# Matmul, GELU, matmul on one Trainium2 core: the first product, too, partly from seven half-size products, with its sums shared out to accumulating DMAs

## Chip, core and metric

The kernel runs on one core of one Trainium2 chip. The metric is device microseconds for one execution; where several runs of a kernel are shown, their median. Inputs and output lie in the chip's main memory (HBM) as float32.

## What is computed

```python
m, k, n, p = 1024, 1024, 2048, 1024          # a: m x k, b: k x n, c: n x p
h = np.matmul(a, b)
h = 0.5 * h * (1 + np.tanh(np.sqrt(2 / np.pi) * (h + 0.044715 * h ** 3)))
return np.matmul(h, c).astype(np.float32)
```

Two products of 1024 x 1024 x 2048 multiply-adds each, with a GELU between them. In the text `h` is the matrix after GELU. Its transpose is what the kernel makes and keeps: `n` on the partitions, `m` along the free dimension, so that it can be the weights of the second product without another transpose.

## The kernel before

TensorE multiplies a 128x128 weight tile by a moving tile of 128 rows and up to 512 columns into PSUM; eight such steps of the contraction over `k`, or over half of `n`, give one 128x512 result. [...] The order on every engine is the order of the program text.

**First product.** `a` is cut into two halves of 512 rows (h = 0, 1). Half 0 arrives through SyncE's queue in four tiles (L74-79), is cast to bf16 by VectorE and ScalarE, and is transposed on TensorE into `aT[0]` (L111-120). The first 768 columns of `b` (`W0`, six tiles of 128) arrive on the same queue, eight loads of 128 rows, 384 KB each (L81-86), into a ring of eight float32 buffers (`b0stage`), and are cast half by VectorE, half by ScalarE (L124-126). L136-143 run over the eight rows of `b` as they arrive, six results side by side in six banks. Everything else comes through GpSimd's queue, which casts float32 to bf16 on the way: a tiny copy on GpSimd that reads the fifth `b` load (`gate`, L94) holds these loads back until then. They are the remaining columns of `b`, the second half of `a`, and `c`. `mm1(t, h)` (L167-172) computes one 128x512 tile of `h` with eight matmuls and has ScalarE apply the GELU from PSUM. In all the first product is 2 x 16 x 8 = 256 matmuls with 512 columns, all bf16. Half 1 of `a` is transposed by `turn(j)` (L185-190) between the last tiles of half 0.

**Second product.** It is already made of seven half-size products instead of eight (the Winograd form of Strassen's method). `h` is seen as 2x2 blocks `h11 h12 / h21 h22` (first index: half of `m`, second: half of `n`), `c` as `c11 c12 / c21 c22`. Sums of blocks take the place of blocks:

- of `h`: `s1 = h21 + h22`, `s2 = s1 - h11`, `s3 = h11 - h21`, and later `s4 = h12 - s2`, in the room of `s2`;
- of `c`: `t1 = c12 - c11`, `t2 = c22 - t1`, `t3 = c22 - c12`, and later `t4 = t2 - c21`, in the room of `t2`.

Each of the seven products is four rows (j) of eight matmuls. Sums are kept in the type float32r (`F32R`), which TensorE multiplies from four-byte data; blocks that need no sum are bf16. All sums are VectorE `tensor_tensor` instructions, issued during the sixteen tiles `mm1(t, 1)` (L235-249) and between the rows of products (L256-259, L263, L266). The order of the products is `h11 c11`, `h12 c21` (three of its four rows), `s2 t2`, `s3 t3`, `s1 t1`, `s4 c22`, `h22 t4`, and at the end the fourth row of `h12 c21` in three narrow pieces. PSUM results are added up by VectorE into `u2` and `u3` and stored through SyncE's queue (`combine`, L294-297).

Of the kernel before, what the change touches and what calls it, by code (L numbers as in the profile page):

```python
# [9 lines left out]
F32 = mybir.dt.float32  # L10
BF16 = mybir.dt.bfloat16
# [8 lines left out]
def kernel(ctx, tc, a, b, c, out):  # L20
    nc = tc.nc
# [8 lines left out]
    W0 = N0 * 128  # L30
    N1 = 4
    W1 = N1 * 128

# [9 lines left out]
    b0stage = ctx.enter_context(tc.tile_pool(name="b0stage", bufs=8))  # L43
# [9 lines left out]
    NH = NT // 2  # L53
    aT = [keep.tile([128, KT, H], BF16, name=f"aT{h}", tag=f"A{h}") for h in range(2)]
    WB = W0 + W1
    b_lo = keep.tile([128, KT, WB], BF16, name="b_lo", tag="B0")
    b_hi = keep.tile([128, KT, N - WB], BF16, name="b_hi", tag="B1")

    def bcols(k0, kn, n0, w):
        if n0 < WB:  # L60
            return b_lo[:, k0:k0 + kn, ds(n0, w)]
        return b_hi[:, k0:k0 + kn, ds(n0 - WB, w)]

    def bt(k, t):
        return bcols(k, 1, t * 128, 128)[:, 0, :]


    hq = [[keep.tile([128, NH, H], F32R if h else BF16, name=f"h{h}{g}") for g in range(2)]
          for h in range(2)]
# [19 lines left out]
    for mt in range(4):  # L89
        load_a0(mt, 2 if mt == 3 else 1)  # L90
# [38 lines left out]
    for mt in range(4):  # L129
        if mt < 3:  # L130
            ab.append(cast_a0(mt + 1))
        turn0(mt, ab[mt], (0,) if mt == 3 else (0, 1))
        if mt < 3:
            warm_up(3)
    cast_b0(0)
    for k in range(KT):  # L136
        if k + 1 < KT:
            cast_b0(k + 1)
        for t in range(N0):
            nc.tensor.matmul(ps[t], bt(k, t), aT[0][:, k, :],  # L140
                             start=(k == 0), stop=(k == KT - 1))
        if k == 0:
            turn0(3, ab[3], (1,))

    def gelu(t, h, p):
        nc.scalar.activation(hq[h][t // NH][:, t % NH, :], p, AF.Gelu_apprx_tanh)  # L146

    for t in range(N0):
        gelu(t, 0, ps[t])


    def load_b(k0, kn, n0, w):
        nc.gpsimd.dma_start(out=bcols(k0, kn, n0, w), in_=bv[:, k0:k0 + kn, ds(n0, w)])

    ps = [(tpool if t < 2 else ppool).tile([128, H], F32, name="pt" if t < 2 else "ps")
          for t in range(N1)]
    for k in range(0, KT, 4):
        load_b(k, 4, W0, W1)
        for i in range(4):
            for t in range(N1):  # L160
                nc.tensor.matmul(ps[t], bt(k + i, N0 + t), aT[0][:, k + i, :],  # L161
                                 start=(k + i == 0), stop=(k + i == KT - 1))
    for t in range(N1):
        gelu(N0 + t, 0, ps[t])


    def mm1(t, h):  # L167
        p = ppool.tile([128, H], F32, name="ps")
        for k in range(KT):
            nc.tensor.matmul(p, bt(k, t), aT[h][:, k, :],  # L170
                             start=(k == 0), stop=(k == KT - 1))
        gelu(t, h, p)

    W2 = 384
    for n0 in range(W0 + W1, N, W2):
        for k in range(0, KT, 4):
            load_b(k, 4, n0, W2)

    a1 = []
    for j in range(4):  # L180
        st = abf.tile([128, K], BF16, name="ab1")
        nc.gpsimd.dma_start(out=st, in_=av[:, 4 + j, :])
        a1.append(st)

    def turn(j):  # L185
        ab = a1[j]
        pt = tpool.tile([128, KT, 128], BF16, name="pt")
        for k in range(KT):
            nc.tensor.transpose(pt[:, k, :], ab[:, ts(k, 128)], ident)  # L189
        nc.vector.tensor_copy(aT[1][:, :, ts(j, 128)], pt)  # L190

    for t in range(N0 + N1, NT):
        mm1(t, 0)
        if t == NT - 3:
            turn(0)
        if t == NT - 2:
            turn(1)
            turn(2)
            turn(3)
# [7 lines left out]
    (h11, h12), (h21, h22) = hq  # L207
    c11 = keep.tile([128, NH, H], BF16, name="c11")
    c21 = keep.tile([128, NH, H], BF16, name="c21")
    c22 = keep.tile([128, NH, H], F32R, name="c22")  # L210
    c12 = keep.tile([128, NH, H], BF16, name="c12", tag="A0")
# [5 lines left out]
    load_c(c11, 0, 0)  # L217
    load_c(c22, 1, 1)
    load_c(c21, 1, 0)
    load_c(c12, 0, 1)  # L220

    t1 = [astage.tile([128, 2, H], F32R, name="t1", tag="a_st") for _ in range(4)]
    t2 = [b0stage.tile([128, 1, H], F32R, name="t2", tag="b0_st") for _ in range(8)]
    s1 = keep.tile([128, NH, H], F32R, name="s1")

    def sum_t1(i):
        nc.vector.tensor_tensor(t1[i], c12[:, ts(i, 2), :], c11[:, ts(i, 2), :], op=SUB)  # L227

    def sum_t2(t):
        nc.vector.tensor_tensor(t2[t], c22[:, t:t + 1, :], t1[t // 2][:, t % 2:t % 2 + 1, :], op=SUB)  # L230

    def sum_s1(t):
        nc.vector.tensor_tensor(s1[:, t, :], h21[:, t, :], h22[:, t, :], op=ADD)

    for t in range(NT):  # L235
        mm1(t, 1)
        if 3 <= t < 7:
            sum_t1(t - 3)
        if 6 <= t < 10:
            sum_t2(2 * (t - 6))  # L240
            sum_t2(2 * (t - 6) + 1)
        if t == WB // 128:
            t3 = keep.tile([128, NH, H], F32R, name="t3", tag="B0")
        if t >= NH + 1:
            sum_s1(t - NH - 1)
        if WB // 128 <= t < WB // 128 + 4:
            i = t - WB // 128
            nc.vector.tensor_tensor(t3[:, ts(i, 2), :], c22[:, ts(i, 2), :], c12[:, ts(i, 2), :], op=SUB)
    sum_s1(NH - 1)

    s2 = [keep.tile([128, NH // 2, H], F32R, name=f"s2{g}", tag=f"A{g}") for g in range(2)]

    def pair(x, i):
        return x[i // 2][:, ts(i % 2, 2), :]

    for i in range(4):  # L256
        nc.vector.tensor_tensor(pair(s2, i), s1[:, ts(i, 2), :], h11[:, ts(i, 2), :], op=SUB)
    for i in range(4):
        nc.vector.tensor_tensor(h21[:, ts(i, 2), :], h11[:, ts(i, 2), :], h21[:, ts(i, 2), :], op=SUB)
    s3 = h21  # L260

    def sum_s4(i):
        nc.vector.tensor_tensor(pair(s2, i), h12[:, ts(i, 2), :], pair(s2, i), op=SUB)  # L263

    def sum_t4(t):
        nc.vector.tensor_tensor(t2[t], t2[t], c21[:, t:t + 1, :], op=SUB)  # L266

    def bank(w=H):
        return ppool.tile([128, w], F32, name="ps", padded_shape=[128, H])

    def prod(p, lhs, rhs, j, q=slice(0, H)):
        for t in range(NH):
            nc.tensor.matmul(p, lhs(t)[:, ts(j, 128)], rhs(t)[:, q],  # L273
                             start=(t == 0), stop=(t == NH - 1))

    def whole(x):
        return lambda t: x[:, t, :]
# [4 lines left out]
    def pairs(x):  # L282
        return lambda t: x[t // 2][:, t % 2, :]

    def ones(x):
        return lambda t: x[t][:, 0, :]

    def new_out():
        return opool.tile([128, H], F32, name="ot")

# [3 lines left out]
    def combine(m, q, p, u, op=ADD, swap=False):  # L294
        ot = new_out()
        nc.vector.tensor_tensor(ot, u if swap else p, p if swap else u, op=op)  # L296
        store(ot, m, q * H)

    R = range(4)
    u2 = [abf.tile([128, H], F32, name="u2", tag="ab1") for _ in R]  # L300
    u3 = keep.tile([128, 4, H], F32, name="u3", tag="B1")

    for j in R:
        p = bank()
        prod(p, whole(h11), whole(c11), j)
        nc.scalar.activation(u2[j], p, AF.Copy)  # L306
    for j in range(3):
        p = bank()
        prod(p, whole(h12), whole(c21), j)
        combine(j, 0, p, u2[j])  # L310
    last = u2[3]
    last_keep = opool.tile([128, H], F32, name="lk", bufs=1)
    nc.gpsimd.tensor_copy(last_keep, last)  # L313
    for j in R:
        p = bank()
        prod(p, halves(s2), ones(t2), j)
        nc.vector.tensor_tensor(u2[j], p, u2[j], op=ADD)
    for j in R:
        p = bank()
        prod(p, whole(s3), whole(t3), j)  # L320
        nc.vector.tensor_tensor(u3[:, j, :], p, u2[j], op=ADD)
        sum_s4(j)
    for j in R:
        p = bank()
        prod(p, whole(s1), pairs(t1), j)
        combine(4 + j, 1, p, u3[:, j, :])
        nc.vector.tensor_tensor(u2[j], p, u2[j], op=ADD)
        sum_t4(2 * j)
        sum_t4(2 * j + 1)
    for j in R:  # L330
        p = bank()
        prod(p, halves(s2), whole(c22), j)
        combine(j, 1, p, u2[j])
    for j in R:
        p = bank()
        prod(p, whole(h22), ones(t2), j)
        combine(4 + j, 0, p, u3[:, j, :], op=SUB, swap=True)
    for q0, w, queue in ((0, 256, nc.sync), (256, 128, nc.scalar), (384, 128, nc.sync)):
        p = bank(w)
        prod(p, whole(h12), whole(c21), 3, q=ds(q0, w))  # L340
        ot = new_out()
        nc.vector.tensor_tensor(ot[:, 0:w], p, last_keep[:, ds(q0, w)], op=ADD)  # L342
# [30 lines left out]
```

## Time and profile before

| | us |
|---|---|
| three runs | 123.58, 123.93, 124.08 |
| median | 123.93 |
| the profiled execution, whole | 123.87 |
| its span, first to last instruction in the profile | 122.1 |

The granted TensorE clock was 1.0 for the whole span. The profile counts the busy time of each engine, but matmuls are pipelined, so "TensorE busy" is not "TensorE at its peak"; the pace at which matmuls follow each other is read from the chain of waits and from the timeline. Three stretches of the span will be spoken of:

| stretch, us from the span's start | what runs | matmuls of 512 columns |
|---|---|---|
| 0 to 21.85 | loads, casts, transposes, first six tiles of `h` | 48 |
| 21.85 to 69.02 | rest of the first product | 208, and 32 transposes |
| 69.02 to 119.2 | second product | 224 (the last eight in 24 narrower pieces) |

The time after 119.2 is the last sum and the store of its result.

### The profile page before, as it was taken

To read this page: it belongs to the slowest core of one execution; us is meant where nothing else is said; L and a number is where in the kernel's file an instruction comes from. 1 tells how busy PE (TensorE), PEld (TensorE's weight loads), DVE (VectorE), ACT (ScalarE), POOL (GpSimd) and SP (SyncE) were. 2 spreads that over 40 slices of the span, in tenths; PEclk is the share of its full clock that TensorE was granted. 3 is DMA by queue.
4 is the path that set the end of the run, shared out by engine and by line. 5 is a ranking of instruction groups with operands and counts; after the bars stand their busy time and mean duration, and the time that the engine had idled before them with its cause. 6 is when DMAs were issued, how large, how long until landed. Compare 5 with 4: busy or idle time off the path is not lost.

```text
span 122.1 us, 1486 instructions
## 1 busy us (share of the span) xinstructions
PE 116.1 (95%) x577; PEld 68.3 (56%) x577; DVE 64.6 (53%) x95; ACT 30.7 (25%) x54; POOL 21.5 (18%) x26
## 2 busy tenths in 40 slices
PE   6977999999998999999999999999999999999990
PEld 2542444444456444444444444468888888888880
DVE  0352340000014200006999999999769999974351
ACT  4454752806331133233323331100000000000000
POOL 2000099132440220000000000797000000000000
PEclk9999999999999999999999999999999999999999
DMA  3999969999999999995000000000600022445425
GB/s 144 351 328 347 413 188 191 198 200 205 209 207 206 329 394 231 206 206 97 0 0 0 5 0 3 3 0 0 258 0 0 5 86 86 157 167 191 163 99 167
DMA packets 12582, 18.44 MB, mean 151 GB/s; under 512 B 800, under 2 KB 7584, under 8 KB 12576
## 3 DMA queue, kind: packets, MB, share of 16 engines
q0 software_dynamic: 7968, 8.91, 39.6%
q1 hardware_dynamic: 4464, 9.37, 20.9%
q10 hardware_dynamic: 144, 0.07, 0.2%
q8 instruction: 4, 0.07, 0.2%
q14 instruction: 2, 0.02, 0.0%
HBM read 20.97 MB, written 4.19 MB: 206 GB/s over the span
## 4 chain that ended last, share of the span: by engine, by line
PE 88%; DMA 6%; SPq 2%; DVE 1%; ACT 0%; issue 0%
PE ps L273 41%; PE ps L170 31%; PE ps L140 8%; DMA b_st<-in_b_dram 6%; PE ps L161 3%; PE pt L161 3%; SPq L78 2%; PE pt L189 1%; DVE aT L190 1%; ACT b_lo L126 0%; SPq L85 0%; DVE ot L342 0%; PE pt L115 0%
## 5 line engine op out<-in xcount | busy, mean ns | idle before, releaser
L146 ACT ACTIVATE h<-ps 128x512 fp32r<-128x512 f32 (+1 forms) x30 | 17.3, 602 | 28.6 <-PE ps L170 26.3
L170 PE MATMUL ps<-aT,b_hi 128*128 128x512 bf16 x96 | 21.4, 379 | 0.0
L170 PE MATMUL ps<-aT,b_lo 128*128 128x512 bf16 x80 | 17.4, 379 | 0.0
L170 PEld LDWEIGHTS <-b_hi 128*128 128x128 bf16 x96 | 9.3, 98 | 10.8
L273 PE MATMUL ps<-t,s 128*128 128x512 f32 x64 | 15.0, 392 | 0.0
L273 PE MATMUL ps<-t,h 128*128 128x512 f32 x64 | 14.8, 389 | 0.0
L273 PE MATMUL ps<-c,h 128*128 128x512 bf16 (+2 forms) x80 | 14.2, 336 | 0.0
L313 POOL COPY lk<-u 128x512 f32<-128x512 f32 x1 | 7.7, 7684 | 33.6 <-ACT u L306 33.6
L273 PEld LDWEIGHTS ps<-t,s 128*128 128x128 f32 x64 | 12.0, 188 | 2.6
L273 PEld LDWEIGHTS ps<-t,h 128*128 128x128 f32 x64 | 12.0, 188 | 2.5
L170 PEld LDWEIGHTS <-b_lo 128*128 128x128 bf16 x80 | 7.8, 98 | 9.4
L227 DVE TENSOR_TENSOR t<-c,c 128x1024 fp32r<-128x1024 bf16 x4 | 4.7, 1222 | 15.8 <-DMA c<-in_c_dram 15.7
L190 DVE COPY aT<-pt 128x1024 bf16<-128x1024 bf16 x4 | 2.7, 689 | 19.4 <-PE pt L189 19.3
L140 PE MATMUL ps<-aT,b_lo 128*128 128x512 bf16 x48 | 10.9, 380 | 0.8 <-DVE b_lo L125 0.8
L273 PEld LDWEIGHTS <-h 128*128 128x128 bf16 x80 | 7.2, 98 | 7.0 <-issue 0.3
L140 PEld LDWEIGHTS <-b_lo 128*128 128x128 bf16 x48 | 4.5, 98 | 6.6 <-DVE b_lo L125 1.1
L215 POOL DMA_DIRECT2D c<-in_c_dram x8 | 5.9, 744 | 11.7 <-PE ps L170 6.0
L296 DVE TENSOR_TENSOR ot<-ps,u 128x512 f32<-128x512 f32 x11 | 7.3, 684 | 1.1 <-PE ps L273 1.1
L101 PE MATMUL ps<-warm 128*128 128x512 bf16 x17 | 6.3, 516 | 1.2 <-DVE warm L49 1.2
L273 PE MATMUL ps<-c,s 128*128 128x512 f32 x32 | 7.4, 389 | 0.0
L273 PEld LDWEIGHTS ps<-c,s 128*128 128x128 f32 x32 | 6.0, 188 | 1.2
L125 DVE CAST b_lo<-b_st 128x384 bf16<-128x384 f32 x8 | 2.9, 368 | 5.1 <-DMA b_st<-in_b_dram 5.1
(40 smaller groups left out, 96.5 us busy)
## 6 DMA issues: line engine op xcount, KB each, us to landing
out_dram<-ot SPq DMA_DIRECT2D x15, 256.0 KB, 2.0
c<-in_c_dram POOLq DMA_DIRECT2D x6, 512.0 KB, 14.8
b_st<-in_b_dram SPq DMA_DIRECT2D x7, 384.0 KB, 8.1
c<-in_c_dram POOLq DMA_DIRECT2D x2, 1024.0 KB, 15.0
a_st<-in_a_dram SPq DMA_DIRECT2D x3, 512.0 KB, 4.1
b_hi<-in_b_dram POOLq DMA_DIRECT2D x4, 384.0 KB, 11.3
b_lo<-in_b_dram POOLq DMA_DIRECT2D x2, 512.0 KB, 7.2
ab<-in_a_dram POOLq DMA_DIRECT2D x4, 256.0 KB, 13.9
```

The costliest lines, as they stand in the source:

```text
L101: nc.tensor.matmul(ps[N0 - 1], warm[:, 0:128], warm, start=True, stop=True)
L125: nc.vector.tensor_copy(b_lo[:, k, 0:HW], b_st[k][:, 0:HW])
L140: nc.tensor.matmul(ps[t], bt(k, t), aT[0][:, k, :], start=(k == 0), stop=(k == KT - 1))
L146: nc.scalar.activation(hq[h][t // NH][:, t % NH, :], p, AF.Gelu_apprx_tanh)
L161: nc.tensor.matmul(ps[t], bt(k + i, N0 + t), aT[0][:, k + i, :], start=(k + i == 0), stop=(k + i == KT - 1))
L170: nc.tensor.matmul(p, bt(k, t), aT[h][:, k, :], start=(k == 0), stop=(k == KT - 1))
L190: nc.vector.tensor_copy(aT[1][:, :, ts(j, 128)], pt)
L215: nc.gpsimd.dma_start(out=dst[:, t:t + 4, :], in_=cv[:, r * NH + t:r * NH + t + 4, ts(q, H)])
L227: nc.vector.tensor_tensor(t1[i], c12[:, ts(i, 2), :], c11[:, ts(i, 2), :], op=SUB)
L273: nc.tensor.matmul(p, lhs(t)[:, ts(j, 128)], rhs(t)[:, q], start=(t == 0), stop=(t == NH - 1))
L296: nc.vector.tensor_tensor(ot, u if swap else p, p if swap else u, op=op)
L313: nc.gpsimd.tensor_copy(last_keep, last)
```

## The change

The half of `h` that belongs to the first 1024 columns of `b` (`h11`, `h21`) is still computed directly, with 64 + 64 matmuls. The other half (`h12`, `h22`) is computed as a 2x2 block product of its own: `a` in halves of `m` and of `k`, the last 1024 columns of `b` in halves of `k` and of `n`. With `bx` for the left two of these four blocks and `b12`, `b22` for the right two, it takes seven products of four rows with four matmuls each, 112 matmuls where there were 128. Its sums are `as1`, `as2`, `as3` (of `a`), `bt2`, `bt3` and the new `b12` (of `b`), all float32r; `a22` is a float32r copy of a block of `aT[1]`, made by ScalarE. The GELU now follows a VectorE sum (`add_gelu`) for these tiles. The core of the diff, first product:

```diff
-    W0 = N0 * 128
+    W0 = N // 2
-    b0stage = ctx.enter_context(tc.tile_pool(name="b0stage", bufs=8))
+    b0stage = ctx.enter_context(tc.tile_pool(name="b0stage", bufs=6))
...
+    nc.gpsimd.dma_start(out=b12, in_=bv[:, 0:KH, W0 + H:N])
+    nc.gpsimd.dma_start(out=b22, in_=bv[:, KH:KT, W0 + H:N])
+    for k in range(0, KT, KH):
+        nc.gpsimd.dma_start(out=bx[:, k:k + KH, :], in_=bv[:, k:k + KH, W0:W0 + H])
...
+        nc.scalar.activation(a22[:, :, ts(j, 128)], aT[1][:, KH:KT, ts(j, 128)], AF.Copy)
...
+    def mm1_half(t, q):
+        p = bank(256)
+        for k in range(KT):
+            nc.tensor.matmul(p, b_lo[:, k, ts(t, 128)], aT[1][:, k, ts(q, 256)],
+                             start=(k == 0), stop=(k == KT - 1))
+        gelu(h21[:, t, ts(q, 256)], p)
...
+    mm1(6, 0, h11[:, 6, :])
+    turn(0)
+    mm1(7, 0, h11[:, 7, :])
+    turn(1)
+    turn(2)
+    mm1_half(0, 0)
+    turn(3)
+    mm1_half(1, 0)
+    mm1_half(2, 0)
+    for t in range(3):
+        mm1_half(t, 1)
...
+    for i in range(2):
+        tt(as1[i], aT[1][:, P2[i], :], aT[1][:, P2[i + 2], :], op=ADD)
...
+    for t in range(3, NH):
+        mm1(t, 1, h21[:, t, :])
...
+    def add_gelu(dst, p, u):
+        ot = new_out()
+        tt(ot, p, u, op=ADD)
+        gelu(dst, ot)
...
+    for j in R:
+        p = bank()
+        prod(p, KH, whole(bx), whole(aT[0]), j)
+        nc.scalar.activation(v2[:, j, :], p, AF.Copy)
+    for j in R:
+        p = bank()
+        prod(p, KH, whole(bx, KH), whole(aT[0], KH), j)
+        add_gelu(h12[:, j, :], p, v2[:, j, :])
+        if j >= 2:
+            sum_t1(j - 2)
+    for j in R:
+        p = bank()
+        prod(p, KH, pairs(bt2), pairs(as2), j)
+        tt(v2[:, j, :], p, v2[:, j, :], op=ADD)
+        if j >= 2:
+            sum_t1(j)
+    for i in range(2):
+        nc.gpsimd.dma_start(out=as2[i], in_=aT[0][:, P2[i + 2], :], accum_op=ADD)
+    for i in range(2):
+        nc.gpsimd.dma_start(out=bt2[i], in_=bx[:, P2[i + 2], :], accum_op=ADD)
+    for j in R:
+        p = bank()
+        prod(p, KH, pairs(bt3), pairs(as3), j)
+        tt(v3[j], p, v2[:, j, :], op=ADD)
...
+    def sum_t2(i):
+        nc.scalar.mul(t2[i], c22[:, P2[i], :], -1.0)
+        nc.gpsimd.dma_start(out=t2[i], in_=t1[:, P2[i], :], accum_op=ADD)
...
+        prod(p, KH, whole(b12), pairs(as1), j)
+        add_gelu(h22[:, 4 + j, :], p, v3[j])
+        tt(v2[:, j, :], p, v2[:, j, :], op=ADD)
...
+        prod(p, KH, whole(b22), pairs(as2), j)
+        add_gelu(h12[:, 4 + j, :], p, v2[:, j, :])
...
+        prod(p, KH, pairs(bt2), whole(a22), j)
+        add_gelu(h22[:, j, :], p, v3[j])
```

`sum_t2(0)` and `(1)` stand ahead of the product `b12 as1`, `sum_t2(2)` and `(3)` after it, `sum_s1(2)` and `(3)` ahead of the last of the seven, `sum_s1(0)` and `(1)` after it.

In the second product the seven products are the same, in another order, and four groups of its sums move from VectorE to DMAs that GpSimd issues and that add their source to what lies in the destination (`accum_op=ADD`), after ScalarE has written the other operand, negated, where the sum is a difference. Signs are chosen so that every such sum is an addition:

```diff
+    for j in R:                                  # p1
+        prod(p, NH, whole(h11), whole(c11), j)
+        nc.scalar.activation(p1[:, j, :], p, AF.Copy)
+    for i in (2, 3, 0, 1):
+        nc.scalar.mul(t3p(i), c12[:, P2[i], :], -1.0)
+        nc.gpsimd.dma_start(out=t3p(i), in_=c22[:, P2[i], :], accum_op=ADD)
+    c21 = keep.tile([128, NH, H], BF16, name="c21", tag="BX")
+    load_c(c21, 1, 0)
+    for j in R:                                  # p5
+        prod(p, NH, pairs(s1), whole(t1), j)
+        nc.scalar.activation(p5[:, j, :], p, AF.Copy)
...
+    for j in R:                                  # p6
+        prod(p, NH, halves(s2), pairs(t2), j)
+        tt(u2[:, j, :], p, p1[:, j, :], op=ADD)
+        tt(p5[:, j, :], u2[:, j, :], p5[:, j, :], op=ADD)
+    for g in range(2):
+        nc.gpsimd.dma_start(out=s2[g], in_=h12[:, ts(g, KH), :], accum_op=ADD)
+    for i in R:
+        nc.gpsimd.dma_start(out=t2[i], in_=c21[:, P2[i], :], accum_op=ADD)
+    for j in R:                                  # p7
+        prod(p, NH, whole(s3), t3t, j)
+        tt(u3[j], p, u2[:, j, :], op=ADD)
+        combine(4 + j, 1, p, p5[:, j, :])
+    for j in range(3):                           # p2
+        prod(p, NH, whole(h12), whole(c21), j)
+        combine(j, 0, p, p1[:, j, :])
+    for j in R:                                  # p3
+        prod(p, NH, halves(s2), whole(c22), j)
+        combine(j, 1, p, p5[:, j, :])
+    for j in R:                                  # p4
+        prod(p, NH, whole(h22), pairs(t2), j)
+        combine(4 + j, 0, p, u3[j])
```

(The names p1 to p7 beside the loops are added here, and the lines that take a bank are left out.) `c21` is loaded only now, into the room of `bx`; before, it was loaded with the rest of `c`. The last row of `h12 c21` in three pieces stays at the end, and GpSimd's copy `lk` (L313) is gone.

## The prediction

> **What bounds the kernel now.** I read the chain that ended last first, by engine and then in order of time, because it says which engine a saved microsecond must come from.
>
> ```profile
> PE 88%; DMA 6%; SPq 2%; DVE 1%; ACT 0%; issue 0%
> ...
> 12.62 9.23 PE ps L140 x42
> ...
> 37.83 0.46 PE pt L189 x8
> 38.30 0.02 issue
> 38.32 0.70 DVE aT L190
> 39.02 0.04 issue
> 39.06 0.61 PE pt L189 x8
> 39.67 29.35 PE ps L170 x136
> 69.02 50.17 PE ps L273 x240
> ```
>
> The reader sees a TensorE that is fed without a gap from 12.62 on, but for 0.7 us at a transpose. A bf16 matmul of 512 columns costs 29.35 / 136 = 0.216 us. So the number of matmuls is the time, and fewer of them is a gain only if nothing else becomes late. Second, the stages of the second product, 32 matmuls each (window, TensorE busy first, DMA share and GB/s last):
>
> ```profile
> 80.76:88.23 7.47, 7.47 (x35) 6.17 (x33) 7.02 (x10) 0.00 (x0) 3.91 (x1) 1.00 0.28 105
> 88.23:95.48 7.25, 7.25 (x33) 6.01 (x32) 5.93 (x7) 0.00 (x0) 0.00 (x0) 1.00 0.00 0
> 95.48:102.73 7.25, 7.25 (x33) 6.01 (x32) 7.25 (x12) 0.00 (x0) 0.00 (x0) 1.00 0.20 75
> ```
>
> Float32r matmuls take 7.25 / 32 = 0.2266 us. VectorE is nearly full here, DMA nearly idle. Third, the loads at the start and VectorE's pitch, from the timeline, and the DMA rate of one window (last number, GB/s):
>
> ```profile
> 15.15 0.38 POOL L94 COPY gate<-b_st 128x1 f32<-128x1 f32 x1 [13.84 <-DMA b_st<-in_b_dram]
> 15.46 1.63 POOL L153 DMA_DIRECT2D b_lo<-in_b_dram  x2
> 17.04 0.36 DVE L125 CAST b_lo<-b_st 128x384 bf16<-128x384 f32 x1 [0.53 <-DMA b_st<-in_b_dram]
> 18.01 0.36 DVE L125 CAST b_lo<-b_st 128x384 bf16<-128x384 f32 x1 [0.61 <-DMA b_st<-in_b_dram]
> ...
> 98.10 0.68 DVE L327 TENSOR_TENSOR u<-ps,u 128x512 f32<-128x512 f32 x1
> 98.70 1.28 DVE L266 TENSOR_TENSOR t<-t,c 128x512 fp32r<-128x512 f32 x2
> ...
> 13.00:14.00 1.00, 1.00 (x6) 0.48 (x5) 0.36 (x1) 0.68 (x2) 0.00 (x0) 1.00 1.04 415
> ```
>
> A 384 KB load lands every 0.97 us at 415 GB/s. A VectorE sum of 512 columns takes 0.60 us of queue (98.10 to 98.70), one of 1024 takes 1.2. GpSimd's DMAs, issued from 15.46 on, first move data at about 17.0: 1.55 us from issue.
>
> **What the Trainium skill says.** "DMA: Bandwidth & Descriptors", SWDGE vs HWDGE: a DMA that accumulates can only be issued by GpSimd. Its section on queues: the sixteen DMA engines take turns between queues, so stores from SyncE's queue and GpSimd's sums share one rate; the trace before has stores alone at that time and can't show it. "Collectives: The Full Stack", "The bandwidth ceiling": an add in the DMA engine costs no cycles of its own, but it reads two sources, and so ran at about half of a copy's rate. No accumulating DMA is in the trace. "SBUF — State Buffer", "Who interferes with whom": a VectorE instruction with two SBUF inputs holds up GpSimd's reads, not its descriptors; the trace shows the first (the copy `lk` took 7.68 us beside a full VectorE), not the second.
>
> **The change, part by part**, against the profiled execution: span 122.1, whole 123.87, which is 0.06 below the median.
>
> *Matmuls.* 256 bf16 matmuls of the first product become 160 bf16 and 80 float32r: 55.2 us become 160 x 0.2158 + 80 x 0.2266 = 52.7. Gain 2.5 us. The 24 matmuls cut into 48 of 256 columns: the last product before took 1.94 us for 24 pieces instead of 1.73 for eight whole ones, 13 ns for each extra piece, so 0.2 to 0.3 us; I take 0.2. Transposes: the stall of 0.7 us goes. In its place `mm1_half(0, 0)` waits for the copy after `turn(1)`, which in the chain ended 1.19 us after that turn began (37.83 to 39.02), with two turns of 0.45 in between: 0.3 us. Counted whole, TensorE needs from the end of the first stage to the end of the first product 16 x 0.2158 (two tiles) + 1.8 + 0.3 (turns) + 5.4 (halves) + 8.6 (five tiles) + 6.9 (`bx`) + 18.1 (float32r) = 44.6 us; before, 69.02 - 21.85 = 47.2.
>
> *The start.* The eight `b` loads grow from 384 to 512 KB. The second half of the first landed at 10.99 and the last at 18.01; the steps grow by a third: 10.99 + 0.33 + 7.02 x 4/3 = 20.7, then a cast of 0.47 and six matmuls, 1.3: 22.5 instead of 21.85. The gate now opens at 16.8, GpSimd's loads move data from 18.65 on (1.85 after the landing, as before), and the last `b` loads share the engines with them for 2 us: between nothing (the last two steps before, 0.97 each, show no slowing) and 1.2 us. I take 0.7. First stage: ends at 23.2, 1.4 late (0.6 to 1.9). Only six buffers: the seventh load waits for a cast at about 12, well before its turn. So the first product ends at 67.9 instead of 69.02: 1.1 us won.
>
> *VectorE.* The twelve sums for the first product, 12 x 1.2 = 14.6 us after the last transposed tile (30.6), are done at 45.2; needed at 49.8. From the first `add_gelu` (47.3) to the start of p5 (74.8) it has 28 sums of 512 and 8 of 1024: 16.9 + 9.6 = 26.5 in 27.5 us. Hidden, with 1 us to spare; six banks carry the delay in between. ScalarE's GELU, copies and eight negations of 1.0 us are under 0.7 per step of 0.9: hidden. `c` arrives before use: GpSimd's loads up to `c22` are 12.6 MB at the 388 GB/s that the casts before reached, done at about 52.
>
> *The sums by DMA* are the question. Price of one of 512 KB destination: it reads 4 KB of old sum and 2 KB of bf16 per partition, 0.79 MB, at 415 GB/s: 1.9 us; with a float32r source 1.05 MB, 2.55 us. That is an estimate (415 from the loads, two reads from the skill). Lower bound: the write alone, 0.52 MB, 1.28. Upper: nothing in the trace sets one; I carry one and a half times the estimate, 2.9, as the end for the range. At 1.9 and 2.55, with 1.55 from issue and 0.5 for landing:
>
> - `as2`, `bt2`: issued when `bt2 as2` ends, 53.4; data from 55.05; `as2` lands 59.4 (needed 61.1), `bt2` 63.2 (needed 64.8). Hidden.
> - `t2`, four at 2.55: done by 75, needed at 82.05. Hidden. GpSimd waits here for ScalarE; nothing else is in its queue.
> - `t3`: negated after p1 (74.8 + 0.6, then 1.0 each), data from 78.0, done 88.2; last needed 89.75. Hidden by a hair. Then `c21`, 2.1 MB, 5.2 us: 93.4, needed 96.55.
> - `s2` (two, each twice the size, 7.6 us) waits on GpSimd for p6 to end (89.3), with the four `t2` sums queued behind it, which wait for `c21` as well; and its data cannot start before the `c21` that was issued ahead of it is through, 93.4. Beside it the stores of p7 and of one row of p2, 5 x 0.63: done 104.2, landed 104.7. Needed by p3's fifth matmul at 102.6: stall 2.1.
> - `t2` again, 7.6 us and five stores, 3.2: 115.0, landed 115.5. Needed at 110.4 + 2.1: stall 3.0.
>
> Sum: 121.0 (122.1 - 1.1) + 5.1 = 126.1 span, 127.9 whole. If the engines overlap reading a store with part of an add, stores cost half: stall about 2.3, 125.1. I take the middle of these weighted to the first: **127.0 us**.
>
> **The rivals.**
>
> 1. *Forecast: adds run at two reads per write*, 0.40. For: the DMA rate of all loads is one number, 415. Range 124.5 to 130.
> 2. *Adds cost their write alone, or the reads hide* (other side: faster). `t3` done 83, `c21` 88.4, `s2` starts only when p6 has ended (91) and lands 99, `t2` 106: no stall. 122.8 us (122.0 to 123.6). The point of decision: 4 x 1.33 + 4 times the bf16 price, `c21` and stores must fit 78.0 to 102.6; that is a price below 1.65 us. Chance 0.28. For: DMA is idle in that stretch before, and the windows are 7 us or more. Against: the skill's two reads.
> 3. *Adds slower than two reads* (2.9 us): `bt2` 2.5 late, `t3` by 5.6 more, `s2` by 7, `t2` by 7: 22 us, 145. At 2.3 us some 133. Chance 0.25.
> 4. *The adds are in time, but VectorE's spare microsecond is not there*, or the start loses all 1.9: PSUM banks come free late, the gain is eaten: 123.5 to 124.8. Chance 0.07.
>
> **From these to numbers.** This kernel's measurement tells 0.5% (0.6 us) from no change. Faster: nine tenths of case 2, 0.25. Same: the rest of 2, the edge of 1, half of 4: 0.13. Slower: 0.62. Range: from 122.4 (most of case 2) to 137 (case 1 and two fifths of case 3); outside are 0.04 below and 0.15 above. The likeliest case's own range is 124.5 to 130.
>
> **What would show it.** First stage ending at 23.2, not 21.85; first product at 67.9 without a DMA in its chain; float32r at 0.2266 us. Accumulating DMAs of 512 KB one after another every 1.9 us (bf16 source) or 2.55. In the chain, a DMA wait at the start of p3 and one at p4, 2 and 3 us. Wrong if p3 and p4 begin on time (rival 2), if TensorE already waits at `b22 as2` or p7 (rival 3), or if a VectorE sum ends the waits (rival 4).

## The result, and the profile after

| | before | changed kernel |
|---|---|---|
| median, us (six runs each) | 123.86 | 129.60 (128.52 to 131.01) |
| ratio, 95% interval | | 1.0449 (1.0403 to 1.0495) |
| profiled execution, whole / span | 123.87 / 122.1 | 128.52 / 126.7 |

The change makes the kernel 4.5% slower. The profiled execution is the fastest of the six, so readings below are of a mild case. The chain that ended last, of the changed kernel, as its page sums it up by engine:

```profile
DMA 33%; issue 32%; PE 21%; POOL 7%; DVE 5%; SPq 1%; POOLq 0%; DVEq 0%
```

and its late pieces in order of time (start, length, what):

```profile
79.44 16.58 DMA c<-in_c_dram
...
97.09 18.79 DMA t<-c
115.88 0.04 issue
115.92 7.98 PE ps L233 x50
```

TensorE's 88% of the chain have become 21%. From 79 to 116 the chain is two waits for GpSimd's queue: for the load of `c21`, and for the last sums, `t4`, which reach TensorE at 115.9. TensorE's timeline, first the start of the second product in the kernel before, then the changed kernel from there on:

```profile
68.86 12.25 PE L273 MATMUL ps<-c,h 128*128 128x512 bf16 x56
```

```profile
66.34 7.08 PE L233 MATMUL ps<-c,h 128*128 128x512 bf16 x31
73.07 14.88 PE L233 MATMUL ps<-t,s 128*128 128x512 f32 x64
87.79 0.61 PE L233 MATMUL ps<-t,h 128*128 128x512 f32 x2
89.29 0.70 PE L233 MATMUL ps<-t,h 128*128 128x512 f32 x2 [0.89 <-DMA t<-c]
...
96.18 5.35 PE L233 MATMUL ps<-c,h 128*128 128x512 bf16 x23
101.18 1.27 PE L233 MATMUL ps<-c,s 128*128 128x512 f32 x4
105.52 8.27 PE L233 MATMUL ps<-c,s 128*128 128x512 f32 x28 [3.07 <-DMA s<-h]
113.62 1.52 PE L233 MATMUL ps<-t,h 128*128 128x512 f32 x6
115.92 6.19 PE L233 MATMUL ps<-t,h 128*128 128x512 f32 x26 [0.78 <-DMA t<-c]
121.95 1.94 PE L233 MATMUL ps<-c,h 128*128 128x256 bf16 x24
```

The reader should first see the good half: p1 begins at 66.34, where the second product began at 68.86 before. Then three waits, each where a product reads a DMA sum for the first time: 0.9 us in p7 (two matmuls, then a pause), 3.1 in p3 and 0.8 in p4. (Counted from where the matmul ahead would have ended at 0.2266 us each, they are 3.4 in p3, from 102.1 to 105.52, and 0.9 in p4. The expectations below say 1.2 for p4, which is the wait of its weight load.) One more loss hides in p3: from 105.52 to p4's first matmul at 113.62 its last 28 matmuls take 8.1 us, where 28 x 0.2266 = 6.3 would do, so 1.8 are lost. (The expectations say 7.88 and 1.5, from a window that cuts the last matmul short.) A window over them gives the cause in its third number from the end, the granted clock, which fell during these matmuls:

```profile
101.20:105.50 4.30, 1.25 (x6) 0.71 (x4) 0.69 (x1) 0.00 (x0) 0.00 (x0) 1.00 1.05 295
105.50:113.40 7.90, 7.88 (x28) 6.31 (x28) 2.08 (x3) 0.00 (x0) 0.00 (x0) 0.78 1.08 302
```

The clock was not low all that time: from 107.1 to 110.4 it was 0.50, before and after that 1.00. Half the pace for some 3.4 us is the 1.8.

So 2.5 us are won in the first product (68.86 - 66.34). From one product's first matmul to the next one's, p7 takes 8.4 us (87.79 to 96.18), p3 12.4 and p4 8.3, where 7.25 would do: 1.1 + 5.2 + 1.1 = 7.4 are lost. 122.1 - 2.5 + 7.4 = 127.0, the span of 126.7 to within 0.3. The DMA engines, nearly idle in these stages before, are at 1.05 and 1.08 in both windows.

### The profile page after: what moved, and what is told of

Same layout as the page of the kernel before. It is cut to its first block, busy times and chain, and to the rows that moved or that the text cites. A ratio compares the mean times of both kernels' runs of the same rounds, so it can differ in the third digit from the quotient of the medians.

```text
span 126.7 us, 1585 instructions
## 1 busy us (share of the span) xinstructions
PE 115.3 (91%) x579; PEld 76.4 (60%) x585; DVE 77.5 (61%) x107; ACT 46.7 (37%) x77; POOL 28.3 (22%) x41
## 4 chain that ended last, share of the span: by engine, by line
DMA 33%; issue 32%; PE 21%; POOL 7%; DVE 5%; SPq 1%; POOLq 0%; DVEq 0%
DMA t<-c 15%; DMA c<-in_c_dram 13%; PE ps L132 8%; PE ps L233 6%; DMA a_st<-in_a_dram 5%; PE ps L174 3%; POOL t L292 2%; POOL bt L283 1%; POOL t3b L356 1%; POOL t L356 1%; DVE aT L161 1%; DVE as L212 1%; PE pt L160 1%; DVE as L210 1%; PE pt L107 1%
## 5 line engine op out<-in xcount | busy, mean ns | idle before, releaser
L342 DVE TENSOR_TENSOR ot<-ps,p 128x512 f32<-128x512 f32 x11 | 7.5, 687 | 15.1 <-DMA out_dram<-ot 15.1
L174 PE MATMUL ps<-aT,b_lo 128*128 128x512 bf16 x54 | 12.5, 379 | 0.1
L241 DVE TENSOR_TENSOR ot<-ps,v 128x512 f32<-128x512 f32 x16 | 10.5, 695 | 3.2 <-PE ps L233 3.2
L138 ACT ACTIVATE h<-ps 128x512 bf16<-128x512 f32 (+2 forms) x19 | 9.4, 536 | 8.3 <-PE ps L174 6.2
L138 ACT ACTIVATE h<-ot 128x512 bf16<-128x512 f32 (+1 forms) x16 | 9.7, 628 | 7.2 <-DVE ot L241 7.2
L132 PE MATMUL ps<-aT,b_lo 128*128 128x512 bf16 x47 | 10.7, 379 | 0.9 <-DVE b_lo L117 0.9
L233 PEld LDWEIGHTS ps<-t,h 128*128 128x128 f32 x48 | 8.9, 188 | 4.2 <-DVE u L369 1.3
L233 PE MATMUL ps<-as,bt 128*128 128x512 f32 x32 | 7.7, 396 | 0.0
L233 PE MATMUL ps<-as,b 128*128 128x512 f32 x32 | 7.4, 389 | 0.0
L117 DVE CAST b_lo<-b_st 128x512 bf16<-128x512 f32 x8 | 3.4, 426 | 6.3 <-DMA b_st<-in_b_dram 6.3
L233 PE MATMUL ps<-aT,bx 128*128 128x512 bf16 x31 | 7.0, 379 | 0.1
```

The lines of the kernel that those rows point to most:

```text
L117: nc.vector.tensor_copy(b_lo[:, k, 0:HW], b_st[k][:, 0:HW])
L132: nc.tensor.matmul(ps[t], b_lo[:, k, ts(t, 128)], aT[0][:, k, :], start=(k == 0), stop=(k == KT - 1))
L138: nc.scalar.activation(dst, src, AF.Gelu_apprx_tanh)
L174: nc.tensor.matmul(p, b_lo[:, k, ts(t, 128)], aT[h][:, k, :], start=(k == 0), stop=(k == KT - 1))
L233: nc.tensor.matmul(p, lhs(t)[:, ts(j, 128)], rhs(t)[:, q], start=(t == 0), stop=(t == n - 1))
L241: tt(ot, p, u, op=ADD)
```

## The experiments

Three theories stood at the start. A: the queue of DMA sums is what is late, because each sum pays for reading two operands. B: the stores meet those DMAs, hold VectorE's four output buffers and so PSUM (VectorE waited 15.1 us for stores). C: VectorE lacks time. All ratios are to the kernel before, run on the same chip beside the experiment.

**What an add costs (e4).** Every DMA sum made a plain DMA, so that the sums are left out.

```diff
-        nc.gpsimd.dma_start(out=as2[i], in_=aT[0][:, P2[i + 2], :], accum_op=ADD)
+        nc.gpsimd.dma_start(out=as2[i], in_=aT[0][:, P2[i + 2], :])
...
```

> Every accumulating DMA becomes a plain one from the same source to the same destination; all twelve-odd sums by DMA are left out, so the output is not the reference's. Theory A (the old sum's read is what is paid): a 512 KB DMA takes about 1.3 us instead of 2.06 (bf16 source) or 2.6 to 3.1 (float32r source), s4 lands near 97, no wait at p7, p3 or p4; span 119.5 to 120, time about 121.5. If what costs is the packet or the conversion, not the second read: DMAs take 2 us or more as before and the waits stay within 1 us of what they were.

Measured: 122.05 us, ratio 0.9871 (0.9837 to 0.9905). From issue to landing (last number, median), the changed kernel first, then e4:

```profile
t<-t POOLq DMA_DIRECT2D x4, 512.0 KB, 8.6
s<-h POOLq DMA_DIRECT2D x2, 1024.0 KB, 15.5
```

```profile
t<-t POOLq DMA_DIRECT2D x4, 512.0 KB, 4.3
s<-h POOLq DMA_DIRECT2D x2, 1024.0 KB, 6.0
```

These times include queueing. The pace is in the landings one after another: the start of a DMA's issue plus its time to landing. The two DMAs of `as2` and the two of `bt2` (first and last start, then least, median and most time to landing), again the changed kernel first, then e4:

```profile
L281 POOL DMA_DIRECT2D as<-aT x2: 906/1054/1202, 51.8 to 52.5; - x2
DMA to landing us min/median/max: 4.1/4.9/5.7
L283 POOL DMA_DIRECT2D bt<-bx x2: 1485/1638/1791, 53.1 to 53.6; - x2
DMA to landing us min/median/max: 7.2/7.9/8.7
```

```profile
L281 POOL DMA_DIRECT2D as<-aT x2: 543/543/543, 52.5 to 53.1; - x2
DMA to landing us min/median/max: 3.3/3.7/4.0
L283 POOL DMA_DIRECT2D bt<-bx x2: 531/531/531, 53.7 to 54.3; - x2
DMA to landing us min/median/max: 4.7/5.0/5.4
```

So in the changed kernel they landed at 55.9, 58.2, 60.2 and 62.3, some 2.1 us each (2.05, counted by the first of the sixteen engines to finish), and the first two `t2` at 64.9 and 68.4; counted by the first engine, 64.4 and 67.0, 2.6. In e4 the same six came every 1.28 us. A write of 0.52 MB in 1.28 us is 410 GB/s; an add with a bf16 source reads 0.79 MB in 2.05 (some 380 GB/s), one with a float32r source 1.05 MB in 2.6 (400 GB/s). Both kinds add the same number of elements, so a price of the adding alone would not tell them apart; the bytes read at the usual rate fit both. e4 itself takes away the read of the old sum and the adding together, and with them every wait of the second product.

**Which sums set which wait (e1, e2).** One group of sums at a time goes back to VectorE. e1 takes s4, one sum after each row of p7; e2 takes t4, in the rows of p2 and once after them.

```diff
-        nc.gpsimd.dma_start(out=s2[g], in_=h12[:, ts(g, KH), :], accum_op=ADD)
...
+        sj = s2[j // 2][:, P2[j % 2], :]
+        tt(sj, h12[:, P2[j], :], sj, op=ADD)
```

> The sum s4 (two DMAs of 1 MB) goes back to VectorE, one 1024-column sum after each row of p7; the other DMA sums stay. Theory A (the DMA engines are full from the end of p1 on, each add pays two reads, and p3 and p4 wait in that queue): 8 us leave the queue, p3 starts without a wait (3.4 us saved, and the 1.5 us that its matmuls lose to the lower clock after the wait), the t2 sums end near 107 and p4's wait of 1.2 goes; the 0.9 before p7 stays. Span 120 to 121 instead of 126.7, time about 122.5. Theory B (the stores and their four buffers hold up VectorE and so PSUM): the waits of p3 and p4 shrink by under 2 us, span 125 or more. Theory C (VectorE has no room here): p7 and p2 grow by up to 4.8 us.

```diff
-        nc.gpsimd.dma_start(out=t2[i], in_=c21[:, P2[i], :], accum_op=ADD)
...
+        tt(t2[j], t2[j], c21[:, P2[j], :], op=ADD)
```

> The sum t4 (four DMAs of 512 KB, the last in the queue) goes back to VectorE, in the rows of p2 and after them; s4 stays a DMA. Theory A: s4 lands as before, at about 105.5, because what is ahead of it in the queue is unchanged; p3 still waits 3 us and runs at the lower clock for a while; only p4's wait of 1.2 us goes. Span about 125.5, time 127.3. Theory B: stores meet no DMA sums after 103, VectorE gets its buffers in time, and p3's wait shrinks too: 123 or less.

Measured: e1 123.41 us, ratio 0.9963 (0.9941 to 0.9986), from 20 runs; e2 128.37, ratio 1.0344 (1.0278 to 1.0409). TensorE's timeline, e1 first, then e2:

```profile
90.11 0.70 PE L233 MATMUL ps<-t,h 128*128 128x512 f32 x2 [0.90 <-DMA t<-c]
...
96.99 5.35 PE L233 MATMUL ps<-c,h 128*128 128x512 bf16 x24
102.00 7.63 PE L233 MATMUL ps<-c,s 128*128 128x512 f32 x32
109.46 7.41 PE L233 MATMUL ps<-t,h 128*128 128x512 f32 x32
```

```profile
102.45 1.26 PE L233 MATMUL ps<-c,s 128*128 128x512 f32 x4
106.78 7.97 PE L233 MATMUL ps<-c,s 128*128 128x512 f32 x28 [3.06 <-DMA s<-h]
114.59 7.41 PE L233 MATMUL ps<-t,h 128*128 128x512 f32 x32
```

Without s4 in the queue p3 and p4 run through, 32 matmuls each without a break, and only p7's 0.9 is left. Without t4 the wait at p3 is what it was, 3.06 us, since nothing ahead of s4 changed; only p4 is rid of its wait. VectorE found room for either group, which speaks against C. Both times are about 1 us above the 122.5 and 127.3 expected, which started from the changed kernel's profile with its early first stage: it ended there at 21.78, here at 22.6 and 23.0.

**Stores (e8).** Six output buffers instead of four.

```diff
-    opool = ctx.enter_context(tc.tile_pool(name="opool", bufs=4))
+    opool = ctx.enter_context(tc.tile_pool(name="opool", bufs=6))
```

> The changed kernel with six instead of four output buffers; nothing else. Theory A: VectorE's waits for stores (15 us in the changed kernel) shrink, but p3 and p4 wait for the same DMA sums as before: time within 1 us of 129.6. Theory B (stores hold VectorE, VectorE holds PSUM): the waits of TensorE at p3 and p4 shrink with VectorE's, 126 or less.

Measured: 129.43 us, ratio 1.0422 (1.0377 to 1.0468). From the list of waits of e8 (engine, line, waited for: total, times, longest):

```profile
PE ps L233 <- DMA s<-h: 3.0, 1, 3.0
...
DVE ot L342 <- DMA out_dram<-ot: 1.2, 1, 1.2
```

VectorE's waits for stores fell from 15.1 to 1.2 us and the time did not move: a long wait off the chain. B falls as a hold-up of VectorE. The stores do share the engines (256 KB took 5.4 us to land, 2.1 in e1), but that acts through the queue.

**The low clock (e9).** Twelve matmuls of zeros between p2 and p3.

```diff
+    p = bank()
+    for _ in range(12):
+        nc.tensor.matmul(p, warm[:, 0:128], warm, start=True, stop=True)
```

> The changed kernel with twelve matmuls of zeros (2.6 us) between p2 and p3, into a bank that is then overwritten, so that TensorE does not stand idle while it waits for s4. Nothing lands earlier. If the wait alone is what costs, the time stays at 129.6 (the idle 3.1 us are only filled). If 1.5 us of the loss at p3 is the lower granted clock that follows the idle time (28 matmuls took 7.88 us there, 6.34 at full clock), the clock stays at 1.0, p3 ends 1.5 us earlier, and part of it is given back at p4's wait for t4, which still lands near 116: time 128.2 to 129.2.

Measured: 129.0 us, ratio 1.0462 (1.0396 to 1.0527), so no difference from the changed kernel can be told. TensorE's timeline:

```profile
105.78 6.64 PE L233 MATMUL ps<-c,s 128*128 128x512 f32 x28 [0.62 <-DMA s<-h]
...
116.19 6.20 PE L233 MATMUL ps<-t,h 128*128 128x512 f32 x26 [1.88 <-DMA t<-c]
```

The clock stayed at 1.0 and p3 ran at full pace from the same landing on, but p4 then waited 1.9 us for t4, landing at 116.1. So in this kernel the clock's 1.8 us was not a cost of its own: the end is set by the last DMA sum, with or without it. Where nothing waits behind it the fall seems to cost time: of e2's four runs the one with a mean clock of 1.0 took 127.13 us, the others, at 0.987 and 0.973, 128.24 to 129.44.

**Rate or order (e3, e5).** Between 72 and 76.7 the DMA engines of the changed kernel stand still, because GpSimd waits for ScalarE's negation of `t3`, which is queued behind p1's copies. e3 fills the gap with the load of `c21`:

```diff
     for i in (2, 3):
         sum_t2(i)
+    c21 = keep.tile([128, NH, H], BF16, name="c21", tag="BX")
+    load_c(c21, 1, 0)
```

> No work is removed: only the load of c21 is issued earlier, right after the last t2 sum of the first group, so that it fills the stretch near 72 to 77 in which the DMA engines stand idle for want of the negated t3 operands. Theory A with capacity enough (it is the order in the queue that is late): t3 starts about 1 us later and p7 waits about 2 us instead of 0.9, but s4 starts at 89 to 90 instead of 94, lands at 100, and p3 and p4 don't wait: span 121 to 122, time about 123.3. If the rate alone were the limit and not the order (theory D): the work pushed past 103 is the same, the waits only move, span within 1.5 us of 126.7.

e5 fills it with the t3 sums themselves, moved ahead of p1 whole:

```diff
+    for i in (2, 3, 0, 1):
+        nc.scalar.mul(t3p(i), c12[:, P2[i], :], -1.0)
+        nc.gpsimd.dma_start(out=t3p(i), in_=c22[:, P2[i], :], accum_op=ADD)
     for j in R:
         p = bank()
         prod(p, NH, whole(h11), whole(c11), j)
```

> All sums stay on DMAs and all of their work is the same. Only the four negations for t3 on ScalarE, each with its DMA, stand ahead of p1's four copies instead of behind them, so that the t3 sums fill the stretch from 72 to 76.6 in which the DMA engines idle. Theory A: first t3 sum starts at 73 instead of 76.6, c21 and s4 follow 3 to 4 us earlier, s4 lands at about 101 against a need near 102, t4 at about 112 against 111: the waits of 0.9 and 3.4 go, of 1.2 some stays; span 120 to 121, time about 122.3. If the rate were the limit however the queue is filled: the waits of p3 and p4 stay at 3 us or more together, 126.

Measured: e3 126.48 us, ratio 1.0191 (1.0126 to 1.0256); e5 125.22, ratio 1.0112 (1.0056 to 1.0169), runs from 124.34 to 126.82. By the ratios they win some 3 and 4 us over the changed kernel with the same DMA work, so its order was part of the loss; neither reaches the 123.3 and 122.3 expected of them. e3, then e5:

```profile
91.82 0.70 PE L233 MATMUL ps<-t,h 128*128 128x512 f32 x2 [1.79 <-DMA t<-c]
92.35 1.55 PE L233 MATMUL ps<-t3b,h 128*128 128x512 f32 x4
93.71 1.91 PE L233 MATMUL ps<-t,h 128*128 128x512 f32 x4
...
105.35 7.63 PE L233 MATMUL ps<-c,s 128*128 128x512 f32 x32
112.81 7.41 PE L233 MATMUL ps<-t,h 128*128 128x512 f32 x32
```

```profile
108.21 1.61 PE L233 MATMUL ps<-t,h 128*128 128x512 f32 x6
111.74 6.19 PE L233 MATMUL ps<-t,h 128*128 128x512 f32 x26 [1.92 <-DMA t<-c]
```

In e3 s4 landed at 100.7 and p3 and p4 ran through. But the last t3 sum landed at 91.7 instead of 89.2, and after the wait for it groups of four matmuls took up to 1.9 us instead of 1.07, at half the clock (0.50 from 92.8 to 96.1). In e5 p7 and p3 run through and the wait has moved to t4, whose last sum landed at 111.7, some 2 us after its reader was ready (108.21 + 6 x 0.2266 = 109.6). So the rate is short as well: the queue holds a little more work than fits, even when it is filled without a gap. e5's runs fall in two groups: three with a mean granted clock of 1.0 took 124.3 to 124.6 us, three at 0.983 to 0.986 took 125.8 to 126.8. What tips a run into one or the other is not shown.

**A version that beats both (e7, e6).** e7 is e1 with the t3 sums in the order in which p7 reads them; e6 is e1 with t3 begun early.

```diff
-    for i in (2, 3, 0, 1):
+    for i in R:
         nc.scalar.mul(t3p(i), c12[:, P2[i], :], -1.0)
```

> e1 with the t3 sums issued in the order in which p7 reads them (0, 1, 2, 3 instead of 2, 3, 0, 1). Theory A: p7's first reads find their sums; the last sum, landing at about 89.9 in e1, is now read 1.4 us after p7's start instead of 0.45, so the wait of 0.9 shrinks to nothing or at most 0.3: time 122.6. If the wait is for something else, it stays: 123.4.

> e5 and e1 together: t3 begun early and s4 on VectorE. Theory A: no DMA wait is left from p5 to the end, span 119.5 to 120.3 by the start's own scatter, time 121.3 to 122.1. If VectorE has become the bound (its row sums, s4 and stores in p7): p7 or p2 longer than 7.25 and 5.2 us, time 123 or more.

Measured: e7 122.28 us, ratio 0.9863 (0.9826 to 0.9899); e6 121.85, ratio 0.9831 (0.9797 to 0.9865). TensorE in e6:

```profile
66.80 7.08 PE L233 MATMUL ps<-c,h 128*128 128x512 bf16 x31
73.53 14.88 PE L233 MATMUL ps<-t,s 128*128 128x512 f32 x64
...
95.51 5.35 PE L233 MATMUL ps<-c,h 128*128 128x512 bf16 x23
100.51 7.63 PE L233 MATMUL ps<-c,s 128*128 128x512 f32 x32
107.98 7.42 PE L233 MATMUL ps<-t,h 128*128 128x512 f32 x32
```

No product waits. The change thus is worth some 2 us of 124, once s4 is taken out of the queue and t3 is begun early (or, in e7, put in order: p7 takes 7.5 us there, 8.4 in e1).

## Why the prediction was right

The forecast was slower, through p3 and p4 waiting for DMA sums that pay two reads; the time fell in its range (122.4 to 137), and in the likeliest case's own (124.5 to 130), 2.6 above the 127.0 given. Step by step:

- **Matmuls.** 44.6 us from the end of the first stage to the end of the first product were forecast. From the second stage's first matmul at 21.62 to p1's at 66.34 the profile has 44.7. Confirmed.
- **The start**: 23.2 was forecast, 1.4 us late (0.6 to 1.9), of which 22.5 came from the larger loads and 0.7 from sharing the engines with GpSimd's loads. The profiled execution had 21.78; the nine profiles of e1 to e9, with the same start, lie between 21.9 and 23.0, around 22.5. So the loads were priced about right and the profiled execution was a lucky one (of the kernel before there is one profile). The 0.7 was nothing: once begun, the 42 matmuls ran without a gap (12.55 to 21.78), and took 9.2 to 9.3 us in the other profiles as well.
- **VectorE hidden with 1 us to spare.** Right: before p7 TensorE waited for no VectorE sum in the first product or in p1 and p5, but for the 0.3 us at `mm1_half` that was forecast. There was room for s4 as well (e1), which the step had not looked for.
- **The price of a sum**: 1.9 and 2.55 forecast, 2.05 and 2.6 measured, and e4 agrees with the reason. The t3 sums were the exception: from their first data at 76.7 to the last landing at 89.2 they took 3.1 us each on average; this made p7 wait 0.9 where the forecast had them "hidden by a hair".
- **s4 and t4.** Landing forecast at 104.7 and 115.5, measured at 105.5 and 115.9. The stalls, 2.1 and 3.0 forecast, were 3.4 and 0.9, plus 1.8 at the lower clock, which the forecast did not have. e9 shows why the division matters little: t4's landing sets the end. That both landings came within 1 us of the forecast is partly luck, since errors cancelled: t3's data began to move 1.3 us sooner than forecast (76.7, not 78.0), but its sums took 2.2 us longer, and `c21` landed at 96.0 (93.4 forecast). Then s4 had less beside it than the five stores of the forecast: VectorE had only one output buffer back before s4 landed (at 101.7) and the second at 105.9. The last section shows why.
- **The sum.** 127.9 came out of the two-read case, and 127.0 was given, by leaning towards stores that cost half. The profiled execution took 128.52, the median 129.6. That lean was the wrong way. (It was itself summed a little high: with stores at half, the terms give stalls of 0.5 and 1.4, 1.9 in all, not 2.3.) Why the other five executions were slower than the profiled one is not shown.
- **The copy `lk`.** Its 7.68 us were read as a sign that VectorE held up GpSimd's reads. The trace has no such copy beside an idle VectorE, so it could not show that.

Rival 2 (a sum costs its write alone) falls with e4, where the write alone takes 1.28 us, rival 3 (slower than two reads) with the landings, rival 4 with e1 and the timeline.

## What to carry to other kernels

An accumulating DMA is not a free adder: price it by the bytes it reads, old sum included, and add up the queue between the first moment its operands exist and the first read, with loads and stores in it, before moving sums off an engine. When such a queue is full, take off it a group that others stand behind (s4 off won 4.9%, t4, behind it, 1%), and start the rest when their room is free, not when program order happens to reach them; here one group of sums back on VectorE and a block moved ahead turned 4.5% slower into 1.7% faster. A long wait on an engine off the chain (VectorE's 15 us for stores) can be removed without any gain.

## What was not expected of the hardware

- The t3 sums landed 2.6 to 3.5 us apart (79.9, 83.0, 85.7, 89.2); by the first engine to finish, the way the 2.6 of the t2 sums was counted, 2.7, 2.6 and 3.4. So it is the last that is out of line, with the load of `c21` right behind it in the queue; in e5, where that is so too, it took 3.5. With `c21` ahead of them (e3) all came 2.5 apart. The plain copies of e4 show it as well (1.5, 1.5 and 2.3 apart, where the others took 1.28), so it isn't the adding. That the load behind it slows it is a guess; the cause stays open.
- After a wait of 3.1 us the granted clock fell to 0.50, not at once but 1.5 us after the matmuls had begun again, and for some 3.4 us (107.1 to 110.4). In e2 and e8 it was at half for as long, from 0.6 us before and from 0.3 us after the matmuls began again. In e3 it fell after 1.8 us, with another 0.8 idle shortly before; after the 1.9 us in e5 it did not, and the 26 matmuls that followed took 6.19. So no single length of a wait decides it in these runs.
- Issuing an accumulating DMA kept GpSimd busy for about 0.9 us (1.82 for two), a plain one in e4 for 0.53 to 0.55.
- Stores and sums shared the engines by packets and not by bytes. While both queues were full, each moved as many packets as the other, but the stores' are the smaller ones. So a store of 256 KB, issued at 92.25, landed only at 101.6, and two stores' worth moved beside s4 where the forecast had five. From 106 to 113 it was 386 packets and 384; e8 and e9 show the same. The changed kernel from 97 to 105, GpSimd's queue (q0) and SyncE's (q1), with packets, MB and the time of the packets as a share of the engines':

```profile
q0 software_dynamic: 290, 1.80, 83.2%
q1 hardware_dynamic: 293, 0.54, 20.5%
```
